# Output projection to second MLP of an encoder trunk: hand-ordered engines, another tile order, early first products

## The chip, the cores and the metric

The kernel runs on one core of one Trainium2 chip. The metric is the device time of one execution in microseconds, as the median of three runs. The core has a matrix engine (TensorE, PE in the profile, with its weight loads as PEld), a vector engine (VectorE, DVE), a scalar engine (ScalarE, ACT), a general engine (GpSimd, POOL) and an engine that issues the DMA transfers (SyncE, SP). Each of them works through its own queue of instructions in order; semaphores between them say when an operand is ready.

## The reference

Two residual layers on 1024 tokens of width 1024, in float32. Layer 0 mixes tokens by pooling, layer 1 by differential attention; each is followed by a gated MLP with a convolution over three neighbouring tokens. What is computed at the place of the change:

```python
h = h + o.reshape(b, s, 1024) @ w_o                 # output projection of the attention, residual
x = rms_norm(h, ffn_norm[1])
g, u = jnp.split(x @ w_up[1], 2, axis=-1)           # 1024 -> 2 x 2816
gc = conv_b + sum(conv_w[j] * shifted(g, j) for j in range(3))
h = h + (gelu(gc) * u) @ w_down[1]
```

## The kernel before

**Number format.** Every float32 matmul operand is split into a rounded part `hi` and a remainder `lo`, and a product is three matmuls: hi x hi, hi x lo, lo x hi. ScalarE makes `hi` (a cast), VectorE or GpSimd makes `lo` (a subtraction). All the large matmuls are 128x128 weights against 512 columns.

**The MLP's up-projection** is done in 22 units of 128 features of g and of u. A unit `j` multiplies two halves of the contraction and two halves of the tokens with seven products instead of eight (a Strassen-like scheme): products 1 to 7, twelve matmuls each, with seven token operands `x[1]` to `x[7]` (built once) and seven weight operands `w[1]` to `w[7]` (built for each unit by the generator `prep(j)`, one piece for each call of `next`). Products 1 and 2 go to one PSUM bank (`up_a`), 6, 7 and 4 to a second (`up_b`), 5 and 3 to a third (`up_c`). VectorE adds them up between the products: `u = b + g` (L511) reads the bank `up_b` after product 6, and product 7, which accumulates in the same bank, comes after it. Then come the convolution (ScalarE L536, VectorE L537 and L540) and, late, in the next unit behind its product 1, `gated(j)`: Gelu on ScalarE and two multiplications on VectorE. In `unit(j)` the products stand in the order 1, 6, 2, 7, 5, 4, 3.

**The seam.** Between the attention and that MLP stands the rest of the output projection (`wo_rest`), token tile by token tile (eight tiles of 128 tokens, in the order of `ORDER`). For each tile: load the partial sum `hs`; two halves of twelve matmuls into two banks (`wo_acc`); VectorE adds each half to `hs` (L176) and ScalarE sums the squares (L177); `rstd` makes the factor of the RMS norm (a sum, a square root on ScalarE, five small VectorE instructions); ScalarE scales the tile into `xs` (L293); TensorE transposes it in eight blocks (`tp`, L300); and `combine` builds the tile's columns of the token operands. A tile t below 4 gives columns of `x[1]` and `x[2]`. A tile t of 4 or more needs tile t - 4 as well and gives columns of `x[6]`, `x[7]`, `x[5]`, `x[4]`, `x[3]`, by three VectorE combinations (L341, L342, L343), a fourth (L345), five casts on ScalarE (L305) and five remainders, two on VectorE and three on GpSimd (L306). Product 1 of any unit needs the four tiles 0 to 3, products 6, 7, 5, 4 and 3 need all eight.

**What sets the order.** Buffers come from pools, and a scheduler places the instructions of the seam and of unit 0 on each engine by its own estimate and by the priorities written in the code. From unit 1 on a hand order holds on TensorE, VectorE and ScalarE (`manual_schedule`): there the engines take their instructions in the order in which the program writes them. GpSimd and the DMA queue are left to the scheduler.

## Time and profile before

| | |
|---|---|
| median of three runs | 2095.46 us (2094.21 to 2097.51) |
| the profiled execution | 2099.03 us, of which the span of the core is 2097.2 us |
| TensorE busy | 2010.8 us, 96% of the span |
| VectorE busy | 1561.3 us, 74% |
| ScalarE busy | 1023.4 us, 49% |
| GpSimd busy | 900.8 us, 43% |
| mean granted TensorE clock | 0.981 |

The profile's page gives shares over the whole span. The seam with its surroundings is a small part of it (about 100 us of 2097), so it has to be read from views that are cut to this stretch: busy time by windows, the chain of work that ended last, and the instructions in order of time on each engine. In the last view a row holds the start in us, the duration in us, engine, line, operation, what is written and what is read, the shapes, and in brackets the idle time of that engine just before, with what ended it.

### The profile page before, as it was taken

How to read it: one execution, taken by the hardware profiler on the slowest of the kernel's cores; microseconds unless marked ns; L12 is line 12 of the kernel's file. 1: busy time of each engine (PE TensorE's matmuls, PEld its weight loads, DVE VectorE, ACT ScalarE, POOL GpSimd, SP SyncE). 2: the span in 40 equal slices, each digit the busy share in tenths (PEclk: the TensorE clock that was granted, in tenths of full speed). 3: DMA queues.
4: the chain of work that ended last, by engine and by line, in shares of the span. 5: the costliest groups of instructions: out<-in, count | busy, mean ns of one | idle time of the engine just before them, and what ended most of it. 6: DMA issues, size and time to landing. Idle time of an engine off the chain costs nothing.

```text
span 2097.2 us, 27633 instructions
## 1 busy us (share of the span) xinstructions
PE 2010.8 (96%) x9659; PEld 1670.2 (80%) x9659; DVE 1561.3 (74%) x2278; ACT 1023.4 (49%) x1834; POOL 900.8 (43%) x689
## 2 busy tenths in 40 slices
PE   5789999999999999999999998987999999999998
PEld 5668888888888877888888886876888888888886
DVE  6877777777775658999989987768667677775665
ACT  6743333333453646666666665556333333344443
POOL 4589999996000000101110111013999999930000
PEclk8889999999999999999999999998999999999999
DMA  4225455454976422122212216243354545458663
GB/s 159 92 77 191 146 161 170 133 188 136 355 231 219 161 66 66 43 69 66 62 45 72 58 38 216 101 163 112 116 170 159 179 143 187 138 190 334 201 210 131
DMA packets 221720, 301.90 MB, mean 144 GB/s; under 512 B 17852, under 2 KB 142092, under 8 KB 218764
## 3 DMA queue, kind: packets, MB, share of 16 engines
q1 hardware_dynamic: 221580, 300.13, 43.7%
q8 instruction: 76, 1.25, 0.2%
q14 instruction: 64, 0.52, 0.1%
HBM read 196.78 MB, written 90.70 MB: 137 GB/s over the span
## 4 chain that ended last, share of the span: by engine, by line
PE 85%; DVE 8%; DMA 3%; ACT 2%; issue 1%; SPq 1%; POOL 0%; ACTq 0%; DVEq 0%; POOLq 0%
PE dn L597 19%; PE up_b L423 17%; PE up_c L423 11%; PE up_a L423 11%; PE pj L1027 7%; PE sc L1113 5%; PE pj L1069 4%; PE po L1155 3%; PE aT L1144 3%; PE pj L1240 2%; PE pp L849 1%; DVE nm L1115 1%; PE pl L829 1%; DMA kf<-t 1%; PE wo_acc L1240 1%
## 5 line engine op out<-in xcount | busy, mean ns | idle before, releaser
L1095 POOL TENSOR_TENSOR q_lo<-qt,q_hi 128x256 fp32r<-128x256 f32 x64 | 49.7, 778 | 685.6 <-ACT q_hi L1094 615.1
L381 POOL TENSOR_TENSOR w_lo<-s,w_hi 128x512 fp32r<-128x512 f32 x168 | 274.1, 1632 | 17.6 <-ACT w_hi L380 17.1
L597 PE MATMUL dn<-hnT_hi 128*128 128x512 f32 x560 | 218.1, 389 | 0.0
L597 PE MATMUL dn<-hnT_hi,hnT_lo 128*128 128x512 f32 x560 | 217.9, 389 | 0.0
L597 PE MATMUL dn<-hnT_lo,hnT_hi 128*128 128x512 f32 x560 | 217.9, 389 | 0.0
L423 PE MATMUL up_b<-x_hi,w_hi 128*128 128x512 f32 x528 | 207.0, 392 | 6.2 <-ACT x_hi L305 4.6
L423 PE MATMUL up_b<-x_lo,w_hi 128*128 128x512 f32 x528 | 206.4, 391 | 2.3 <-DVE x_lo L306 2.3
L381 POOL TENSOR_TENSOR w_lo<-raw,w_hi 128x512 fp32r<-128x512 f32 x130 | 195.1, 1501 | 30.7 <-ACT w_hi L380 26.4
L423 PE MATMUL up_b<-x_hi,w_lo 128*128 128x512 f32 x528 | 206.0, 390 | 0.0
L380 ACT CAST w_hi<-s 128x512 fp32r<-128x512 f32 x176 | 108.4, 616 | 178.7 <-PE up_b L423 87.4
L1115 DVE TENSOR_REDUCE nm<-sc 128x1 f32<-128x1024 f32 x128 | 155.8, 1217 | 15.1 <-PE sc L1113 14.1
L580 ACT CAST hnT_hi<-mst 128x1024 fp32r<-128x1024 f32 (+1 forms) x76 | 74.7, 983 | 169.1 <-PE dn L597 130.6
L581 DVE TENSOR_TENSOR hnT_lo<-mst,hnT_hi 128x1024 fp32r<-128x1024 f32 (+1 forms) x76 | 86.5, 1138 | 92.3 <-ACT hnT_hi L580 92.1
L1118 ACT ACTIVATE prob<-sc,nm 128x1024 f32<-128x1024 f32 x128 | 142.7, 1115 | 21.7 <-DVE nm L1115 11.4
L423 PE MATMUL up_a<-hnT_hi,w_hi 128*128 128x512 f32 x352 | 139.1, 395 | 1.4 <-ACT g L500 0.9
L423 PE MATMUL up_a<-hnT_lo,w_hi 128*128 128x512 f32 x352 | 138.7, 394 | 0.1
L423 PE MATMUL up_a<-hnT_hi,w_lo 128*128 128x512 f32 x352 | 138.5, 393 | 0.0
L395 POOL TENSOR_TENSOR s<-raw 128x512 f32<-128x512 f32 x84 | 133.1, 1584 | 10.4 <-DMA raw<-in_ffn_w_up_dram 4.2
L423 PE MATMUL up_c<-hnT_hi,w_lo 128*128 128x512 f32 x352 | 137.0, 389 | 0.3 <-DVE w_lo L381 0.3
L423 PE MATMUL up_c<-hnT_hi,w_hi 128*128 128x512 f32 x352 | 136.9, 389 | 0.0
L423 PE MATMUL up_c<-hnT_lo,w_hi 128*128 128x512 f32 x352 | 136.9, 389 | 0.0
L423 PEld LDWEIGHTS up_b<-x_hi,w_hi 128*128 128x128 f32 x528 | 99.5, 189 | 29.5 <-ACT x_hi L305 5.5
(296 smaller groups left out, 5455.2 us busy)
## 6 DMA issues: line engine op xcount, KB each, us to landing
raw<-in_ffn_w_up_dram SPq DMA_DIRECT2D x88, 512.0 KB, 4.3
mst<-m_dram SPq DMA_DIRECT2D x70, 512.0 KB, 5.7
wd<-in_ffn_w_down_dram SPq DMA_DIRECT2D x22, 1024.0 KB, 6.1
wd_dram<-wd SPq DMA_DIRECT2D x22, 1024.0 KB, 6.5
m_dram<-cm SPq DMA_DIRECT2D x80, 256.0 KB, 5.6
wst<-wd_dram SPq DMA_DIRECT2D x40, 512.0 KB, 4.8
m_dram<-gc SPq DMA_DIRECT2D x66, 256.0 KB, 6.3
wst<-in_ffn_w_down_dram SPq DMA_DIRECT2D x30, 512.0 KB, 6.6
```

Source lines behind the costliest of these rows:

```text
L380: A.copy(hi, src)
L381: eng.tensor_tensor(lo, src, f32(hi), ALU.subtract)
L395: eng.tensor_tensor(t, a, b, op)
L423: PE.matmul(acc, l[a][:, k], r[b][:, k], start=first and n == 0, stop=n == 11, skip_group_check=True)
L580: A.copy(h_, x)
L581: V.tensor_tensor(l_, x, f32(h_), ALU.subtract)
L597: PE.matmul(banks[t], l[:, q, cols], r[:, q], start=first and cnt == 0, stop=stop and cnt == 3 * n - 1, skip_group_check=True)
L1027: PE.matmul(acc, l[:, k % 2, h], r[:, k], start=(n == 0), stop=(n == 3 * NK - 1))
L1069: PE.matmul(acc, l[:, k % 4], r[:, k], start=(n == 0), stop=(n == 3 * NK - 1))
L1113: PE.matmul(sc[:, ns_], l[:, c], ks[:, c, ns_], start=(l is qhi), stop=(l is qlo))
L1115: V.tensor_reduce(nm, sc, AX.X, ALU.max, negate=True)
L1118: A.activation(soft[j, i][c], sc, AF.Exp, bias=nm, accum_out=sm[:, c, i:i + 1])
```

## The change

Only the seam and the first two units of the second MLP are written anew; the layer before is the same.

- The order of the tiles becomes 0 4 1 5 2 3 6 7.
- A class `Normed` holds one tile and cuts its work into `add`, `scale`, `turn`, `take`, `combine` and `combine2`. A loop over the tiles writes them with a lag: while the matmuls of tile k are issued, tile k-1 is scaled and transposed, and tile k-2 is taken from PSUM and combined.
- The hand order now begins at the seam, and holds for GpSimd too, from there to the last unit. The DMA queue is still left to the scheduler.
- Behind the last tile's matmuls stand products 1 of unit 0, then the last tile's transposes, then product 2 of unit 0 and products 1 and 2 of unit 1 (`start`); the units leave them out later. So unit 0 begins with product 6, and behind it comes product 7 at once; the same in unit 1.
- Weights: the raw weights of units 0 and 1 are loaded into the buffers `wd` and `cm`, which are free there; `w[1]` and `w[2]` of unit 0 are made during tiles 3, 6 and 7, in buffers of the pool `s`, which becomes nine buffers of 512 columns instead of four of 1024; the first two sums of unit 0's weights move from VectorE to GpSimd; the pieces of unit 1's weights come one step earlier.

```diff
-ORDER = (0, 4, 1, 5, 2, 6, 3, 7)
+ORDER = (0, 4, 1, 5, 2, 3, 6, 7)
...
-                self.s = pool(self.es_s, "s", bufs=4, side="right")
+                self.s = pool(self.es_s, "s", bufs=9, side="right")
+                self.s_shape = [P, 512]
...
+    class Normed:
+        def add(self, n, acc):
+            hs = self.h[:, n * 512:(n + 1) * 512]
+            V.tensor_tensor(hs, acc, hs, ALU.add)
+            A.activation(acc, hs, AF.Square, accum_out=self.ss[:, n:n + 1])
+        def scale(self):
+            r = rstd(self.ss)
+            self.xs = self.ar.tile("gc", [P, D], F32, "xs")
+            A.mul(self.xs, self.h, r)
+            nc.sync.dma_start(h_dram[3 * self.layer][self.tt], self.h)
...
+        def take(self):
...
+            for k in range(4):
+                A.mul(self.b12[:, k], self.pts[0][:, k], gcol[:, 2 + self.layer, k:k + 1])
+            self.gained(1, self.b22)
+        def combine(self):
+            G = nc.gpsimd
+            if self.tt < 4:
+                self.put(1, self.u, V)
+                self.put(2, self.v, G)
+                return
+            self.t3 = self.ar.tile("u2", [P, 4, P], F32, "t3")
+            V.tensor_tensor(self.t3, self.b22, self.b12, ALU.subtract)
+            V.tensor_tensor(self.b12, self.b12, self.b11, ALU.subtract)
+            V.tensor_tensor(self.b11, self.t3, self.b11, ALU.add)
+            self.put(6, self.b11, V)
+        def combine2(self):
+            G = nc.gpsimd
+            if self.tt < 4:
+                return
+            self.put(7, self.t3, G)
+            V.tensor_tensor(self.b21, self.b21, self.b11, ALU.subtract)
+            self.put(5, self.b12, V)
+            self.put(4, self.b21, G)
+            self.put(3, self.b22, G)
...
+        def start(j, i):
+            if i == 1:
+                a = ar.tile("ps_dn" if man and j == 1 else "ps_up", [P, 512], F32, "up_a")
+                product(j, 1, a, True)
+                g = ar.tile("g", [P, S], F32, "g")
+                A.copy(half(g, 0), a)
+                pre[j, 1] = a, g
+            else:
+                product(j, 2, pre[j, 1][0], False)
+                pre[j, 2] = True
...
-    each_with_lag(ORDER, wo_rest, lambda: next(mlp))
+    man.enter_context(tc.manual_schedule(engines=ENGINES | {mybir.EngineType.Pool}))
...
+    for k, tt in enumerate(ORDER):
+        p, pp = at(k - 1), at(k - 2)
+        acc = wo_half(tt, 0)
+        if pp:
+            pp.take()
+        if p:
+            p.scale()
+        tiles[tt].add(0, acc)
+        acc = wo_half(tt, 1)
+        if pp:
+            pp.combine()
+        tiles[tt].add(1, acc)
+        if pp:
+            pp.combine2()
+        if p:
+            p.turn()
+        if k == 0:
+            api["load"](0)
+            first, after = api["prep"](0), api["prep"](1)
+            api["next"] = after
+        elif k == 2:
+            api["load"](1)
+        elif k > 4:
+            next(first)
+    p, pp = at(7), at(6)
+    api["start"](0, 1)
+    pp.take()
+    p.scale()
+    pp.combine()
+    p.turn()
+    next(after)
+    api["start"](0, 2)
+    p.take()
+    p.combine()
+    next(first)
+    api["start"](1, 1)
+    pp.combine2()
+    p.combine2()
+    for _ in first:
+        pass
+    api["start"](1, 2)
```

How this moves the instructions shows at three places. In the rows below `rt` is the square root of the norm, `wo_acc,ss<-hs` the sum of squares of one half, `x_hi` and `hnT_hi` are casts of token operands, `w_hi` of weight operands, `b`, `t` and `xf` the tiles that are combined.

ScalarE in the middle of the tile loop, before: the square root of a tile stands between single casts.

```order
L177 ACTIVATE wo_acc,ss<-hs 128x512
L293 ACTIVATE xs<-hs,rs_r 128x1024
L305 CAST x_hi<-xf 128x4x128
L305 CAST hnT_hi_69<-b_13784 128x4x128
L305 CAST x_hi<-xf 128x4x128
L177 ACTIVATE wo_acc,ss<-hs 128x512
L305 CAST hnT_hi_67<-xf 128x4x128
L191 ACTIVATE rt<-ss,eps 128x1
L305 CAST hnT_hi_67<-xf 128x4x128
L177 ACTIVATE wo_acc,ss<-hs 128x512
L293 ACTIVATE xs<-hs,rs_r 128x1024
```

The same engine after, at tile 3: between the last sum of squares and the square root of the same tile now stand the four casts of tile 5 and one cast of a weight.

```order
L365 ACTIVATE wo_acc,ss<-hs 128x512
L383 CAST x_hi<-xf 128x4x128
L365 ACTIVATE wo_acc,ss<-hs 128x512
L383 CAST x_hi<-t_13862 128x4x128
L383 CAST hnT_hi_69<-b_13825 128x4x128
L383 CAST x_hi<-xf 128x4x128
L383 CAST hnT_hi_69<-b_13826 128x4x128
L459 CAST w_hi<-raw_13535 128x512
L191 ACTIVATE rt<-ss,eps 128x1
L370 ACTIVATE xs<-hs,rs_r 128x1024
```

ScalarE at the last tile, before: the copy `g<-up_a` of unit 0's product 1 stands behind the last tile's square root and scaling.

```order
L177 ACTIVATE wo_acc,ss<-hs 128x512 x2
L305 CAST hnT_hi_67<-xf 128x4x128 x2
L191 ACTIVATE rt<-ss,eps 128x1
L293 ACTIVATE xs<-hs,rs_r 128x1024
L332 ACTIVATE b_14074<-tp,gcol 128x128 x4
L500 COPY g<-up_a 128x512
```

After: that copy, and four reads of tile 6's transposes, stand ahead of the last tile's square root.

```order
L365 ACTIVATE wo_acc,ss<-hs 128x512
L578 COPY g<-up_a 128x512
L403 ACTIVATE b_14046<-tp,gcol 128x128 x4
L191 ACTIVATE rt<-ss,eps 128x1
L370 ACTIVATE xs<-hs,rs_r 128x1024
L383 CAST x_hi<-xf 128x4x128
```

VectorE at unit 0, before: the sum `u<-up_b,g` stands ahead of the last weight remainder, and the sum `s` and remainders of a single tile are ahead of it.

```order
L345 TENSOR_TENSOR xf<-xf 128x512
L306 TENSOR_TENSOR x_lo<-xf,x_hi 128x4x128
L306 TENSOR_TENSOR hnT_lo_70<-b_14074,hnT_hi_69 128x4x128
L381 TENSOR_TENSOR w_lo<-s,w_hi 128x512
L395 TENSOR_TENSOR s<-raw,s 128x512
L381 TENSOR_TENSOR w_lo<-s,w_hi 128x512
L381 TENSOR_TENSOR w_lo<-raw,w_hi 128x512
L511 TENSOR_TENSOR u_14156<-up_b,g 128x512
L381 TENSOR_TENSOR w_lo<-s,w_hi 128x512
```

After: ten instructions of the token operands of tiles 6 and 7 and of all of unit 0's remaining weights stand ahead of it.

```order
L423 TENSOR_TENSOR xf<-xf 128x512
L384 TENSOR_TENSOR hnT_lo_70<-b_14046,hnT_hi_69 128x4x128
L423 TENSOR_TENSOR xf<-xf 128x512
L384 TENSOR_TENSOR hnT_lo_70<-b_14104,hnT_hi_69 128x4x128
L474 TENSOR_TENSOR s<-raw_13535 128x512
L460 TENSOR_TENSOR w_lo<-s,w_hi 128x512 x2
L460 TENSOR_TENSOR w_lo<-raw_13535,w_hi 128x512
L474 TENSOR_TENSOR s<-raw_13535,s 128x512
L460 TENSOR_TENSOR w_lo<-s,w_hi 128x512
L608 TENSOR_TENSOR u_14207<-up_b,g 128x512
```

More of the change, by code (lines that the diff above doesn't have):

```diff
@@ L362, in each_with_lag, with ffn @@
         late()
-    def ffn(layer, ar, tail, extra=None):
+    def ffn(layer, ar, tail, extra=None, api=None, man=None):
         G = nc.gpsimd
@@ L495, in unit @@
                 load_down(1)
-            a = ar.tile("ps_up", [P, 512], F32, "up_a")
-            product(j, 1, a, True)
-            g = ar.tile("g", [P, S], F32, "g")
-            A.copy(half(g, 0), a)
+            if (j, 1) not in pre:
+                start(j, 1)
+            a, g = pre[j, 1]
             if late:
@@ L513, in unit @@
             step()
-            product(j, 2, a, False)
+            if (j, 2) not in pre:
+                start(j, 2)
             next(side, None)
@@ L710, in down_all @@
             return ends[2:]
-        load(0)
-        first = prep(0)
-        next(first)
-        if layer:
-            next(first)
-        yield
-        load(1)
-        for _ in first:
-            pass
-        unit(0, prep(1))
-        load(2)
-        with tc.manual_schedule(engines=ENGINES):
+        if api is not None:
+            api.update(load=load, prep=prep, start=start)
+            yield
+            unit(0, api["next"])
+            load(2)
             for j in range(1, NF):
@@ L726, in ffn @@
                 load(j + 2)
+            man.close()
+        else:
+            load(0)
+            first = prep(0)
+            next(first)
+            yield
+            load(1)
+            for _ in first:
+                pass
+            unit(0, prep(1))
+            load(2)
+            with tc.manual_schedule(engines=ENGINES):
+                for j in range(1, NF):
+                    unit(j, prep(j + 1))
+                    load(j + 2)
         ar.open_down()
```

93 lines of the change are left out of this document (70 added, 23 removed).

## The prediction

> **What bounds the kernel now.** I first cut the busy time into windows around the seam, from the first `wo_acc` matmul (1386.73) on.
>
> ```profile
> core 0: us, PE busy (x) PEld busy (x) DVE busy (x) ACT busy (x) POOL busy (x), PEclk, DMA share, GB/s
> 1386.73:1451.00 64.27, 54.38 (x250) 43.90 (x248) 49.11 (x96) 39.93 (x85) 20.17 (x14) 0.92 0.40 131
> 1451.00:1487.34 36.34, 32.68 (x129) 24.71 (x129) 22.25 (x32) 18.23 (x31) 23.18 (x16) 0.92 0.29 87
> 1487.34:1525.00 37.66, 37.66 (x166) 31.20 (x167) 27.05 (x27) 13.65 (x20) 37.03 (x24) 1.00 0.47 153
> 1900.00:2000.00 100.00, 100.00 (x443) 82.80 (x442) 58.47 (x65) 42.65 (x54) 0.00 (x0) 1.00 0.70 245
> ```
>
> From 1487.34 on TensorE is busy without a gap, at full clock; before that it idles and is slowed. The seam can therefore only move the time by moving that moment. The chain of waits and TensorE's instructions in order of time show what it is:
>
> ```profile
> 1487.34 3.02 PE up_b L423 x12
> 1490.35 2.72 PE up_c L423 x12
> ```
>
> ```profile
> 1404.28 1.09 PE L300 MATMUL tp<-ident,xs 128*128 128x128 f32 x8 [0.75 <-ACT xs L293]
> 1405.13 0.48 PE L1240 MATMUL wo_acc<-wo_l,hnT_lo 128*128 128x512 f32 x1
> 1436.77 1.97 PE L300 MATMUL tp<-ident,xs 128*128 128x128 f32 x8 [2.67 <-ACT xs L293]
> 1448.42 1.97 PE L300 MATMUL tp<-ident,xs 128*128 128x128 f32 x8 [4.15 <-ACT xs L293]
> 1452.44 0.63 PE L423 MATMUL up_a<-hnT_hi,w_lo 128*128 128x512 f32 x1
> 1452.87 0.63 PE L423 MATMUL up_a<-hnT_hi,w_hi 128*128 128x512 f32 x1
> 1487.34 0.50 PE L423 MATMUL up_b<-x_hi,w_hi 128*128 128x512 f32 x1 [0.34 <-DVE u L511]
> ```
>
> The last row is product 7 of unit 1, released by `u` (L511) of unit 1. Call this moment R; from the first `wo_acc` matmul it is 1487.34 - 1386.73 = 100.6 us away. Before R stand 192 matmuls of `wo_acc`, ten products of twelve (unit 0's seven and products 1, 6, 2 of unit 1) and 64 transposes. A product takes 2.72 us, and eight transposes hold TensorE for 0.85 (1404.28 to 1405.13): 26 x 2.72 + 8 x 0.85 = 77.5. So 23.1 us are lost: 9.9 + 3.7 = 13.6 idle (the windows), and 9.5 in stretches at half clock, where matmuls follow each other at 0.43 (1452.44, 1452.87) instead of 0.227 us.
>
> **What the change does to this.** The matmuls before R are the same: the units still have ten products before product 7 of unit 1, in another order (products 1 and 2 of both units come first). If nothing were lost, the gain would be 23 us. I place the new order's instructions one after the other on each engine, with these durations:
>
> ```profile
> 1396.95 0.16 DVE L197 SCALAR_TENSOR_TENSOR rs_q<-rs_p,rt 128x1 f32<-128x1 f32 x1
> 1397.15 0.16 DVE L199 SCALAR_TENSOR_TENSOR rs_r<-rs_q,rt 128x1 f32<-128x1 f32 x1
> ...
> 1463.59 0.68 DVE L306 TENSOR_TENSOR x_lo<-xf,x_hi 128x512 fp32r<-128x512 f32 x1
> 1464.19 0.68 DVE L306 TENSOR_TENSOR hnT_lo<-b,hnT_hi 128x512 fp32r<-128x512 f32 x1
> ```
>
> ```profile
> 1428.11 0.62 ACT L305 CAST x_hi<-xf 128x512 fp32r<-128x512 f32 x1 [1.08 <-DVE xf L343]
> 1428.63 0.61 ACT L305 CAST hnT_hi<-b 128x512 fp32r<-128x512 f32 x1
> 1434.44 0.60 ACT L177 ACTIVATE wo_acc<-hs 128x512 f32<-128x512 f32 x1 [0.71 <-DVE hs L176]
> 1435.57 1.15 ACT L293 ACTIVATE xs<-hs,rs_r 128x1024 f32<-128x1024 f32 x1 [0.41 <-DVE rs_r L199]
> 1437.98 1.14 ACT L332 ACTIVATE b<-tp,gcol 128x128 f32<-128x128 f32 x4 [0.76 <-PE tp L300]
> 1442.34 0.29 ACT L191 ACTIVATE rt<-ss,eps 128x1 f32<-128x1 f32 x1 [1.74 <-DVE ss L189]
> ```
>
> ```profile
> 1424.46 1.30 POOL L306 TENSOR_TENSOR hnT_lo<-b,hnT_hi 128x512 fp32r<-128x512 f32 x1 [5.15 <-ACT hnT_hi L305]
> 1425.73 1.80 POOL L306 TENSOR_TENSOR x_lo<-t,x_hi 128x512 fp32r<-128x512 f32 x1
> ...
> 1470.21 1.29 POOL L395 TENSOR_TENSOR s<-raw 128x512 f32<-128x512 f32 x1 [4.18 <-DMA raw<-in_ffn_w_up_dram]
> ...
> 1473.96 1.30 POOL L395 TENSOR_TENSOR s<-raw 128x512 f32<-128x512 f32 x1
> 1475.21 1.30 POOL L395 TENSOR_TENSOR s<-raw,s 128x512 f32<-128x512 f32 x1
> ```
>
> ```profile
> 1425.70 0.68 DVE L342 TENSOR_TENSOR b<-b,xf 128x512 f32<-128x512 f32 x1
> 1426.42 1.66 DVE L343 TENSOR_TENSOR xf<-t,xf 128x512 f32<-128x512 f32 x1
> ```
>
> So in a row VectorE takes 0.60 for a 512-column instruction and 0.20 for a small one, ScalarE 0.52 for a cast, 0.64 for a square with its read-out (estimate from the 0.60), GpSimd 1.25. The last two fences show one more price: a VectorE instruction with both inputs in SBUF and a GpSimd instruction do not run together. GpSimd's at 1425.73 took 1.80 beside VectorE's L342, and VectorE's L343, issued at 1426.42, ended only 0.55 after GpSimd's end at 1427.53. They take turns; a turn of both is 1.25 + 0.60 = 1.85.
>
> *The tile loop.* Between a tile's last matmul and its own transposes TensorE has 0.85 + 5.44 = 6.3 us of other work. For tiles 0, 4, 1, 2 and 6 the chain add, square, sum, root, five small instructions, scaling fits or nearly fits into this (stalls 0.2 and 0.5 by the same placing). For tile 5 it does not, since tile 4's `combine` and `combine2` stand in it: 1.4 until VectorE is through with the remainder of `x[6]`, add 0.7, square 0.65, two casts 1.1, 0.8 until GpSimd's remainder ends, VectorE's remainder and two reads 1.8, sum 0.2, root and reciprocal 0.55, 0.65 until GpSimd's next remainder ends and three small ones 0.6, scaling 1.2: 9.6, a stall of 3.3. For tile 3 the same, with a weight cast (0.5) and one more turn of both (1.85): 12.0, a stall of 5.7. Sum of the loop: 9.7.
>
> *The last tile.* Product 1 of unit 0 starts 1.0 late, because tile 3's remainder stands behind an add. Then tile 7's transposes: the square root waits on ScalarE behind the copy of that product, which only starts 0.2 after the product's end: 0.2 + 0.5 copy + 1.1 reads of tile 6 + 0.3 root + 0.8 small ones + 1.2 scaling = 4.1. Together 5.1. Before, the root stood ahead of the copy.
>
> *Product 7 of unit 0.* Time 0 is the end of tile 7's transposes. TensorE has products 2, 1', 2' (those of unit 1) and 6: until 10.9. Product 7 needs VectorE's `u` of unit 0. VectorE: reads of tile 7 and three combinations until 5.4, behind a GpSimd turn (ScalarE's reads end at 2.4, GpSimd's weight remainder at 3.4), cast and remainder of `x[6]` 6.7, weight 6 at 7.3. Then the ten instructions of the last listing above, beside GpSimd's six remainders of tiles 6 and 7 and two sums of unit 1: the first 0.6, eight turns 14.8: 22.7; the cast of the last weight 0.8, its remainder 0.6, `u` 0.7: 24.8. TensorE waits 13.9. In the order before, `u` of unit 0 was not last of the row, and GpSimd had no work for unit 1 then, because unit 1's raw weights had not arrived (the 4.18 at 1470.21). That wait for a DMA goes, and its work comes in the worst place.
>
> *Product 7 of unit 1.* It needs `u` of unit 1, which stands behind the Gelu of unit 0:
>
> ```profile
> 1476.16 0.69 DVE L533 TENSOR_TENSOR g<-up_b,g 128x512 f32<-128x512 f32 x1 [2.03 <-PE up_b L423]
> 1478.65 1.45 DVE L537 SCALAR_TENSOR_TENSOR gc<-g,convp,gc 128x1023 f32<-128x1023 f32 x1 [1.80 <-ACT gc L536]
> 1480.62 1.71 DVE L540 SCALAR_TENSOR_TENSOR gc<-g,convp,gc 128x1023 f32<-128x1023 f32 x1
> 1485.08 0.69 DVE L475 TENSOR_TENSOR gc<-up_a,gc 128x512 f32<-128x512 f32 x1 [2.75 <-ACT gc L474]
> 1486.60 0.68 DVE L511 TENSOR_TENSOR u<-up_b,g 128x512 f32<-128x512 f32 x1
> ```
>
> From the reading of product 4 (1476.16) to R are 11.2 us. TensorE covered them with four products (10.9), hence the idle 0.34. In the new order two of the four, 1 and 2 of unit 1, are already done; products 3 and 6 cover 5.4. A wait of 5.8 takes the place.
>
> *The DMA queue* I cost at nothing. Unit 0's raw weights take the place of an early load of the same size, unit 1's go out while the first tile runs; a tile's `hs` follows the store of the tile three places ahead:
>
> ```profile
> 1393.96 0.32 SPq L294 DMA_DIRECT2D h_dram<-hs  x1
> 1398.52 0.32 SPq L1361 DMA_DIRECT2D hs<-h_dram  x1
> ```
>
> 4.6 for the store and about as much for the load are under the 16 us between the two tiles' uses; with unit 1's loads beside them the margin is still some 4 us.
>
> *Sum.* Lost after: 9.7 + 5.1 + 13.9 + 5.8 = 34.5, at full clock. Before: 23.1, slow clock included: + 11.4. The clock comes on top. After the idle of 2.67 the transposes took 1.97, not 1.09, and after that of 4.15 the slow stretch lasted from 1448.42 past 1452.87. Three of the new waits (5.7, 13.9, 5.8) are followed by work that R or the end hangs on; from the trace's 9.5 us, lost in three such stretches (at the seam's start and behind the two idles), one costs 3.2. The bounds are 0 and 9.5; I take 4, below the middle, since part falls into waits that are there anyway. Result: + 15.4. The profiled execution took 2099.03 (its span 2097.2 and 1.8 around it), so 2114.4; it lay 3.6 above the median of the runs, 2095.46. On the median: 2111.
>
> On the clock the Trainium skill ("TensorE: Matmul & The Clock Gate", Part 1) says that the clock falls to half after an idle window of about 3.4 us, and returns after as long a busy one. The trace disagrees on the first: 2.67 us were enough. By the page a wait costs an estimated 1.7 us, three cost 5.1, and the sum would be 2112 on the median.
>
> **Rivals.**
> - *Faster.* The place is VectorE's row ahead of unit 0's `u`. If VectorE and GpSimd hardly held each other there (as the rows at 1463.59 and 1464.19, back to back at 0.60), `u` would come at 7.3 + 6.0 + 0.8 + 0.7 = 14.8, the tile loop would lose some 5 less, and lost time is 9.7 - 5 + 5.1 + 3.9 + 5.8 = 19.5; where the ten are also ready early enough that TensorE does not wait for `u` at all, 15.6, which is 7.5 less than now: 2088. It decides from a wait under 3 us there. Against it: the rows at 1425.73 and 1426.42. Chance 0.09.
> - *No change.* The stalls of the loop are only those of the loop before (2.67 and 4.15), and the row ahead of `u` is held half as often: 34.5 - 2.9 - 7.4 = 24.2, 1.1 more than now, and little clock: 2097. Chance 0.13.
> - *GpSimd becomes the bound.* Fourteen of its instructions lie between tile 7 and the last sum of unit 1, whose cast stands on ScalarE ahead of unit 0's convolution. At 1.80 each (1425.73) they end at 7.9 + 25.2 = 33.1, as late as product 4 at 24.8 + 8.2 = 33.0; with the cast 1.4 more than the forecast, and the whole 9.5 of the clock: 11.4 + 1.4 + 9.5 = 22.3, or 2118. Chance 0.15.
> - *The forecast*, between 2102 and 2118: 0.63.
>
> **Numbers.** 0.2% or 4.2 us is about what a measurement of this kernel can tell from no change. Slower by more: 0.63 + 0.15 = 0.78; within: 0.12; faster: 0.10, 0.01 of the second rival counted there. The range reaches down through the no-change case to 2094 and up to 2119, just over the GpSimd case: it leaves out the faster case and the upper half of that one, under 2 in 10.
>
> **What would show it.** Right: in the profile after, TensorE busy without a gap only from about 1500 on; an idle of 10 us or more ahead of an `up_b` matmul, released by `u`; a second of about 6; idles at `tp` of 3 to 6, released by `xs`; VectorE instructions of 1.7 to 1.9 us ahead of `u`. Wrong: the ten instructions at 0.6 to 0.7 each, or the four products ahead of product 6 following at once on tile 6's transposes. The forecast falls if the wait ahead of unit 0's product 7 is under 5 us.

## The result, and the profile after

The changed kernel takes 2112.14 us (median of four runs, 2109.24 to 2116.04), the kernel before 2094.84 in the same session: a ratio of 1.0079 (95% interval 1.0065 to 1.0094), 17.3 us slower. The forecast was 2111.

The profiled execution lasted 2109.24 with a span of 2107.5, which is only 10.3 more than the span before. The difference is in front of the seam: the first `wo_acc` matmul came 7.6 earlier than in the profile of before, although nothing was changed there.

The first `wo_acc` matmul and the first `dn` matmul, TensorE in order of time, before:

```profile
1386.73 1.05 PE L1240 MATMUL wo_acc<-wo_l,hnT_hi 128*128 128x512 f32 x2
1879.15 0.39 PE L597 MATMUL dn<-hnT_hi 128*128 128x512 f32 x1
```

and after, with every idle of TensorE in between up to R (product 7 of unit 1):

```profile
1379.12 0.63 PE L1346 MATMUL wo_acc<-wo_l,hnT_hi 128*128 128x512 f32 x2
...
1412.23 1.10 PE L378 MATMUL tp<-ident,xs 128*128 128x128 f32 x8 [2.98 <-ACT xs L370]
1430.72 1.97 PE L378 MATMUL tp<-ident,xs 128*128 128x128 f32 x8 [3.96 <-ACT xs L370]
1446.24 1.09 PE L378 MATMUL tp<-ident,xs 128*128 128x128 f32 x8 [3.90 <-ACT xs L370]
1455.12 0.50 PE L508 MATMUL up_a<-hnT_hi,w_hi 128*128 128x512 f32 x1 [0.72 <-ACT g L578]
1471.41 0.77 PE L508 MATMUL up_b<-x_hi,w_hi 128*128 128x512 f32 x1 [10.55 <-DVE u L608]
1492.04 0.77 PE L508 MATMUL up_b<-x_hi,w_hi 128*128 128x512 f32 x1 [5.25 <-DVE u L608]
...
1889.66 0.39 PE L695 MATMUL dn<-hnT_hi 128*128 128x512 f32 x1
```

So two stretches are to be compared. I call them the seam (first `wo_acc` to R) and the units (R to the first `dn`). The seam took 1492.04 - 1379.12 = 112.9 where it took 100.6: + 12.3. The units took 397.6 where they took 391.8: + 5.8. Together 18.1; what lies behind `dn` is alike to 0.2 (217.8 against 218.0). That the two medians differ by 17.3 fits this, and not the 10.3 of the spans.

Busy time by windows, after:

```profile
core 0: us, PE busy (x) PEld busy (x) DVE busy (x) ACT busy (x) POOL busy (x), PEclk, DMA share, GB/s
1379.12:1451.00 71.88, 61.03 (x279) 50.09 (x278) 46.20 (x100) 40.59 (x90) 21.16 (x16) 0.93 0.43 139
1451.00:1492.04 41.04, 24.52 (x100) 19.24 (x99) 25.68 (x26) 15.16 (x24) 24.36 (x17) 0.87 0.16 52
1525.00:1600.00 75.00, 75.00 (x329) 61.08 (x328) 56.88 (x52) 26.58 (x40) 63.58 (x43) 1.00 0.49 162
```

Of the seam's 112.9, 77.5 are work; 10.85 + 16.52 = 27.4 are idle, and the remaining 8.0 went in half clock. Before it was 13.6 and 9.5. The last row looks like full work at full clock, and yet is not without a gap. The gaps are too small for the busy column; the chain of waits shows them, one in the product 7 of each unit (2.96 us for a product that takes 2.72):

```profile
1548.70 2.72 PE up_a L508 x12
1551.42 2.96 PE up_b L508 x12
...
1570.70 2.95 PE up_b L508 x12
```

The unit lasts 1570.70 - 1551.42 = 19.28, where seven products are 19.04. Asked for the waits of the weight loads in the units, the trace after names `u` nineteen times (6.5 us in all, 0.5 the longest); before, it names none behind R:

```profile
PEld up_b L508 <- DVE u L608: 6.5, 19, 0.5
```

What makes `u` late are two VectorE instructions of the chain ahead of it: the first part of the convolution (L537 in the kernel before, L635 in the changed one) and the second multiplication of `gated` (L476 and L561). One unit before, VectorE and the GpSimd instructions that begin ahead of each of the two:

```profile
1535.92 1.31 DVE L537 SCALAR_TENSOR_TENSOR gc<-g,convp,gc 128x1023 f32<-128x1023 f32 x1 [1.31 <-ACT gc L536]
1541.54 1.01 DVE L476 TENSOR_TENSOR gc<-u,gc 128x512 f32<-128x512 f32 x1
```

```profile
1534.85 1.29 POOL L381 TENSOR_TENSOR w_lo<-s,w_hi 128x512 fp32r<-128x512 f32 x1
1540.70 1.30 POOL L395 TENSOR_TENSOR s<-raw 128x512 f32<-128x512 f32 x1
```

and one unit after:

```profile
1542.59 2.29 DVE L635 SCALAR_TENSOR_TENSOR gc<-g,convp,gc 128x1023 f32<-128x1023 f32 x1 [1.32 <-ACT gc L634]
1548.92 1.78 DVE L561 TENSOR_TENSOR gc<-u,gc 128x512 f32<-128x512 f32 x1
```

```profile
1542.50 1.30 POOL L460 TENSOR_TENSOR w_lo<-raw,w_hi 128x512 fp32r<-128x512 f32 x1
1548.86 1.29 POOL L460 TENSOR_TENSOR w_lo<-raw,w_hi 128x512 fp32r<-128x512 f32 x1 [0.57 <-ACT w_hi L459]
```

Before, GpSimd's instructions began 1.07 and 0.84 ahead of VectorE's; after, they begin 0.09 and 0.06 ahead, and VectorE's take 0.98 and 0.77 longer. The unit shown is one of the shortest before: over 18 units behind R, L537 took 1.28 to 2.24, and L476 took 0.99 to 1.79, in eleven of them 1.78 or 1.79 as after. What never came before is both of them long in one unit. Their sum was 2.27 to 3.66, without a wait for `u`; after, it is 4.03 to 4.20 in the 19 units that wait, by 0.32 to 0.48 each, and 2.94 in the last one, which doesn't wait.

### The profile page after: what moved, and what is told of

Same layout as the page of the kernel before. It is cut to its first block, busy times and chain, and to the rows that moved or that the text cites. A ratio compares the mean times of both kernels' runs of the same rounds, so it can differ in the third digit from the quotient of the medians.

```text
span 2107.5 us, 27591 instructions
## 1 busy us (share of the span) xinstructions
PE 2014.7 (96%) x9659; PEld 1670.6 (79%) x9659; DVE 1571.4 (75%) x2276; ACT 1021.5 (48%) x1834; POOL 875.5 (42%) x691
## 4 chain that ended last, share of the span: by engine, by line
PE 85%; DVE 7%; ACT 3%; DMA 2%; issue 1%; SPq 1%; POOL 0%; ACTq 0%; DVEq 0%; POOLq 0%
PE dn L695 19%; PE up_b L508 17%; PE up_c L508 11%; PE up_a L508 11%; PE pj L1133 7%; PE sc L1219 5%; PE pj L1175 4%; PE po L1261 3%; PE aT L1250 2%; PE pj L1346 2%; PE wo_acc L1346 1%; PE pp L955 1%; DVE nm L1221 1%; PE pl L935 1%; ACT prob L1224 1%
## 5 line engine op out<-in xcount | busy, mean ns | idle before, releaser
L460 POOL TENSOR_TENSOR w_lo<-s,w_hi 128x512 fp32r<-128x512 f32 x168 | 248.1, 1482 | 57.4 <-ACT w_hi L459 57.2
L460 POOL TENSOR_TENSOR w_lo<-raw,w_hi 128x512 fp32r<-128x512 f32 x130 | 188.3, 1449 | 44.2 <-ACT w_hi L459 44.2
L508 PEld LDWEIGHTS up_b<-x_hi,w_hi 128*128 128x128 f32 x528 | 100.4, 190 | 49.1 <-ACT w_hi L459 10.9
```

The lines of the kernel that those rows point to most:

```text
L460: eng.tensor_tensor(lo, src, f32(hi), ALU.subtract)
L508: PE.matmul(acc, l[a][:, k], r[b][:, k], start=first and n == 0, stop=n == 11, skip_group_check=True)
```

## The experiments

All ran against the kernel before, which took 2090.5 to 2091.1 in these sessions. Seam and units in us, from the trace of one execution of each run:

| run | median us | ratio to before (95%) | seam | units |
|---|---|---|---|---|
| before (first profile) | | 1 | 100.6 | 391.8 |
| changed kernel again | 2111.12 | 1.0097 (1.0082 to 1.0111) | 112.9 | 396.8 |
| before, GpSimd by hand in the units | 2098.03 | 1.0040 (1.0027 to 1.0052) | 100.5 | 398.9 |
| GpSimd to the scheduler from unit 1 | 2146.58 | 1.0271 (1.0257 to 1.0285) | 114.7 | 433.8 |
| two weight steps moved in the units | 2133.65 | 1.0202 (1.0188 to 1.0217) | 114.0 | 418.3 |
| unit 0's weights stepped, with unit 1's | 2113.16 | 1.0112 (1.0096 to 1.0127) | 116.9 | 398.0 |
| unit 0's weights stepped, unit 1's behind | 2106.39 | 1.0075 (1.0061 to 1.0089) | 110.8 | 397.2 |
| root ahead of reads and remainders | 2113.62 | 1.0116 (1.0102 to 1.0130) | 117.7 | 397.6 |
| root ahead of remainders | 2108.94 | 1.0084 (1.0069 to 1.0098) | 110.7 | 397.6 |
| unit 1 without early products | 2109.52 | 1.0086 (1.0072 to 1.0100) | 115.4 | 396.1 |
| remainders to VectorE | 2109.06 | 1.0082 (1.0069 to 1.0095) | 115.2 | 395.9 |
| old tile order | 2111.87 | 1.0099 (1.0085 to 1.0113) | 115.3 | 397.7 |
| three edits together | 2100.34 | 1.0046 (1.0032 to 1.0060) | 106.0 | 396.3 |

The seam varies by itself. Two runs that leave the program of the seam as it is (GpSimd to the scheduler from unit 1; two weight steps moved) show 114.7 and 114.0, where the changed kernel shows 112.9 twice; in both, tile 3's stall is 5.25 or 5.26 instead of 3.96. So a seam that is 2 us longer or shorter says little more than this, and the waits have to be read beside it. Of the edits to the seam, only the three together have an interval of the ratio that lies apart from that of the changed kernel (1.0082 to 1.0111).

My theory: the 12.3 at the seam are what the prediction named (stalls behind the root, the row ahead of `u`, the Gelu without cover), and of the 5.8 in the units, 1.2 are product 7 of unit 1 at half clock behind its wait, and 4.6 are GpSimd's handmade order. The rivals: the units are late because unit 1 enters late; and at the seam there is one bound, so that any edit only moves the waits.

**The changed kernel again.**

> The changed kernel itself, as the measure for the three others of this call. Both theories expect the ratio of the result, 1.008 (1.0065 to 1.0094): some 17 us over the kernel before. If the seam and the units are the whole of it, its trace shows 112.9 us from the first wo_acc matmul to product 7 of unit 1, give or take 1.5, and 397.8 from there to the first dn matmul.

As expected: the ratio's interval overlaps that of the result, the seam is 112.9 again, and the units 396.8. The median is 20.6 above the kernel before, where the two stretches give 17.2; the rest lies elsewhere or in the spread of the runs (2108.09 to 2115.49). The units show where the wait for `u` begins. In the first three of this trace the sum of L635 and L561 is 3.07, 3.63 and 3.85, and nothing waits; in the next 16 it is 4.05 to 4.07, and each has a wait of 0.33 to 0.35.

**GpSimd by hand in the kernel before.** Only the engines of the hand order change:

```diff
-        with tc.manual_schedule(engines=ENGINES):
+        with tc.manual_schedule(engines=ENGINES | ({mybir.EngineType.Pool} if layer else set())):
```

> The kernel before, with GpSimd put in program order from unit 1 of the second MLP on, and nothing else. Theory A (GpSimd's handmade order costs the units): product 7 of most units waits 0.2 to 0.5 us for u, a unit takes 19.27, and the time rises by about 20 x 0.23 = 4.6, to 2099.5 or so from 2095. Rival B (the late entry at the seam does it): the seam is the old one, so the units stay at 19.04 and the time at 2095.

The seam stays at 100.5, the units rise by 7.1 to 398.9, the time by 0.40%. Waits of the weight loads (two of the 21 lie ahead of R, in a stretch that begins at the seam; behind R they are 19 and 7.8 us), and VectorE in one unit:

```profile
PEld up_b L423 <- DVE u L511: 8.8, 21, 1.4
```

```profile
1607.66 2.30 DVE L537 SCALAR_TENSOR_TENSOR gc<-g,convp,gc 128x1023 f32<-128x1023 f32 x1 [1.31 <-ACT gc L536]
1614.00 1.78 DVE L476 TENSOR_TENSOR gc<-u,gc 128x512 f32<-128x512 f32 x1
```

2.30 and 1.78 with the old seam: the handmade order of GpSimd does it, not the late entry. It costs more here than I had expected (4.6), since unit 2 waits 1.21 and 0.95 besides.

**GpSimd back to the scheduler.** The hand order of GpSimd ends behind unit 0:

```diff
-            for j in range(1, NF):
-                unit(j, prep(j + 1))
-                load(j + 2)
             man.close()
+            with tc.manual_schedule(engines=ENGINES):
+                for j in range(1, NF):
+                    unit(j, prep(j + 1))
+                    load(j + 2)
```

> The changed kernel, but GpSimd's order is by hand only up to unit 0 of the second MLP; from unit 1 on it is left to the scheduler, as before the change. In the changed kernel's trace product 7 of every unit from 2 to 21 waits about 0.33 us for VectorE's u (L608), and a unit takes 19.27 us where it took 19.04. Theory A: it is GpSimd's handmade order that does this (its remainders fall on the convolution and the Gelu of VectorE); then the units go back to 19.04, the 0.33 waits go, and the time falls by 19 x 0.23 = 4.2: 2108 where the changed kernel has 2112. Rival B: the units are late because unit 1 enters its Gelu late at the seam and never catches up, whatever GpSimd's order; then the waits of 0.33 stay and the time stays at 2112. Up to the start of product 7 of unit 1 (R) nothing changes by either.

Both theories missed: the units take 433.8. Waits of the weight loads in the units, and GpSimd in order of time:

```profile
PEld up_c L508 <- POOL w_lo L460: 28.3, 14, 3.1
```

```profile
1617.90 1.29 POOL L474 TENSOR_TENSOR s<-raw 128x512 f32<-128x512 f32 x1 [5.78 <-DMA raw<-in_ffn_w_up_dram]
```

The scheduler now gives GpSimd another order than before the change; it stands still for a raw weight and its remainders come late for TensorE. Why that load comes late I did not follow. So this run says nothing on the two theories, only that "left to the scheduler" is not one order.

**Two weight steps moved.** In units 1 to 21:

```diff
-            step()
+            moved = man and j
+            if not moved:
+                step()
             b = ar.tile("ps_up", [P, 512], F32, "up_b")
             product(j, 6, b, True)
...
             next(side, None)
             step()
+            if moved:
+                step()
...
-            step()
+            if not moved:
+                step()
             gc = ar.tile("gc", [P, S], F32, "gc")
             A.activation(gc, g, AF.Identity, bias=cv[:, 3, j:j + 1], scale=cv[:, 1, j:j + 1])
             V.scalar_tensor_tensor(gc[:, 1:], g[:, :S - 1], cv[:, 0, j:j + 1], gc[:, 1:], ALU.mult, ALU.add)
+            if moved:
+                step()
```

> The changed kernel, with GpSimd in program order as it is, but in units 1 to 21 two of the weight steps are written elsewhere: the one ahead of product 6 behind u, and the one ahead of the convolution behind its first VectorE instruction (L635 there). Theory (in the units it is not the handmade order as such that costs 0.23 a unit but two collisions: GpSimd's remainder starts 0.1 ahead of L635, which takes 2.29 instead of 1.3, and another falls on L561, 1.78 instead of 1.0, so that u comes late for product 7): L635 goes back to 1.3 or L561 to 1.0 to 1.2, product 7 no longer waits, a unit takes 19.04 and the time falls by about 4. Rival: GpSimd's instructions only move on to other VectorE instructions of the same chain; 0.2 to 0.3 a unit stays and the time is within 1.5 of the changed kernel.

The convolution's collision goes (1.28), and yet the units take 21.5 us more than in the changed kernel of that session. VectorE's convolution and ScalarE behind it, in one unit:

```profile
1611.05 1.28 DVE L640 SCALAR_TENSOR_TENSOR gc<-g,convp,gc 128x1023 f32<-128x1023 f32 x1 [1.31 <-ACT gc L639]
```

```profile
1615.75 0.62 ACT L459 CAST w_hi<-s 128x512 fp32r<-128x512 f32 x1 [4.23 <-POOL s L474]
...
1616.76 1.06 ACT L559 ACTIVATE gc<-gc 128x1024 f32<-128x1024 f32 x1
```

The Gelu (L559) stands behind a cast that waits 4.23 for GpSimd's sum, and product 7 waits 1.35 for `u` in a unit, although the sum of L640 (the convolution here) and L561 is only 3.06. So collisions are one way in which GpSimd's order makes `u` late, and a cast on ScalarE behind a GpSimd sum is another; a better place for the steps was not found.

**Unit 0's weights behind `u`.** First try: each step of unit 0 (`both`) advances the weights of unit 0 and those of unit 1.

```diff
-    for _ in first:
-        pass
     api["start"](1, 2)
+    api["next"] = both(first, after)
```

> The changed kernel, but the last four weights of unit 0 (w7, w5, w4, w3) are not all made ahead of unit 0; they go out in unit 0's own steps, behind u. Theory (VectorE's row ahead of u is what product 7 of unit 0 waits for): six of the instructions ahead of u go, at a turn of 1.70 each; u comes about when product 6 ends, and product 7 waits only for w7 (sum, cast, remainder, some 4 us) instead of 10.55. R moves 6 ahead and the time falls to about 2106. Rival: the row only moves; the same remainders then stand ahead of the readings and the convolution of unit 0, the wait of 5.25 ahead of unit 1's product 7 grows by as much, and the time stays at 2112 within 2.

Neither: product 7 waits 7.86 now for a cast, unit 1's wait is 7.36, and the seam is 4 longer. TensorE, and ScalarE at that place:

```profile
1469.73 0.79 PE L508 MATMUL up_b<-x_hi,w_hi 128*128 128x512 f32 x1 [7.86 <-ACT w_hi L459]
```

```profile
1468.54 1.66 ACT L459 CAST w_hi<-s 128x512 fp32r<-128x512 f32 x3 [7.13 <-POOL s L474]
```

ScalarE had unit 1's cast in front, which waits for GpSimd's sum; unit 0's `w[7]` stood behind it. Second try: the seven steps of unit 0 (`shared`) advance unit 0's weights in the first four, unit 1's in the last six:

```diff
-    for _ in first:
-        pass
+    next(first)
     api["start"](1, 2)
+    api["next"] = shared(first, after)
```

> The changed kernel, but w5, w4 and w3 of unit 0 are made in unit 0's own steps behind u, and unit 1's weights one step behind unit 0's (so that no sum of GpSimd for unit 1 stands ahead of unit 0's w7 on ScalarE, as it did in the run before). Theory (the row of VectorE ahead of u is what product 7 waits for): four turns of 1.70 go, the wait of 10.55 becomes about 4, R comes 6 earlier and the time falls by 5 to 7 against the changed kernel. Rival (GpSimd's row of six remainders and two sums is the bound behind it): product 7 of unit 0 starts earlier, but the wait ahead of unit 1's product 7 or a weight of unit 1 grows by the same; within 2 of the changed kernel.

```profile
1468.79 0.77 PE L508 MATMUL up_b<-x_hi,w_hi 128*128 128x512 f32 x1 [4.15 <-DVE u L608]
1491.68 0.76 PE L508 MATMUL up_b<-x_hi,w_hi 128*128 128x512 f32 x1 [6.20 <-DVE u L608]
```

The first wait falls from 10.55 to 4.15, as the theory had it; the second grows by 0.95, and tile 3's stall was 5.26 here, not 3.96. So the row ahead of `u` was the cause of that wait. What it pays alone is less sure: R comes 2.1 earlier, the median is 4.7 lower, and the intervals of the two ratios overlap.

**The root ahead.** First try: the root and the scaling of a tile ahead of the reads (`take`) and of `combine2` of the tiles before, `combine2` one tile later (`p3` is the tile three places back; `at(5)` is tile 3, which has no `combine2`).

```diff
         acc = wo_half(tt, 0)
+        if p:
+            p.scale()
+        if p3:
+            p3.combine2()
         if pp:
             pp.take()
-        if p:
-            p.scale()
...
-        if pp:
-            pp.combine2()
...
     p, pp = at(7), at(6)
+    p.scale()
+    at(5).combine2()
     api["start"](0, 1)
     pp.take()
-    p.scale()
```

> The changed kernel, but in the tile loop and behind it the square root, the small instructions and the scaling of a tile stand ahead of the reads and remainders of the tiles before it (combine2 follows one turn later). Theory (the waits of 2.98, 3.96 and 3.90 ahead of the transposes of tiles 5, 3 and 7 come from the remainders that stand ahead of the root): these three waits go, with them some 3 us at half clock; tile 7's transposes come 10 earlier, VectorE's row behind them moves along, and R and the end come 8 to 12 earlier: about 2102. Rival: VectorE's and GpSimd's row of remainders is a bound of its own, since it is now put off; u of unit 0 comes no earlier, the wait ahead of product 7 grows from 10.55 to 18 or more, and the time stays within 3 of 2112.

```profile
1430.95 1.94 PE L378 MATMUL tp<-ident,xs 128*128 128x128 f32 x8 [5.40 <-DVE xf L388]
```

A new wait took the place of the old: tile 3's transposes wait for their PSUM bank, which the reads (L388) give back too late now. Second try, with `take` first again and `combine2` put off. Behind the loop the edit also writes product 1 of unit 0, with the copy that reads it, behind the last tile's scaling.

```diff
         if pp:
             pp.take()
         if p:
             p.scale()
+        if p3:
+            p3.combine2()
...
-        if pp:
-            pp.combine2()
...
     p, pp = at(7), at(6)
-    api["start"](0, 1)
     pp.take()
     p.scale()
+    at(5).combine2()
+    api["start"](0, 1)
```

> The changed kernel, but a tile's last remainders (combine2) are put off until the next tile's root and scaling are out; the reads of the transposes keep their place. (The run before put the reads off too, so the transposes waited for their bank: that wait of 5.4 took the place of the others.) Theory (the waits of 2.98, 3.96 and 3.90 at the transposes come from the remainders that stand ahead of the root): they fall under 1.5 each, the last tile's transposes come 7 to 10 earlier and the time falls by 6 to 10. Rival (VectorE and GpSimd are the bound behind the last tile, with the same row put off): u of unit 0 comes no earlier than 92.3 after the first wo_acc matmul, its wait grows to 18, and the time stays within 2 of the changed kernel.

```profile
1416.43 1.09 PE L378 MATMUL tp<-ident,xs 128*128 128x128 f32 x8 [2.98 <-ACT xs L370]
1424.15 1.09 PE L378 MATMUL tp<-ident,xs 128*128 128x128 f32 x8 [1.16 <-ACT xs L370]
1434.41 1.09 PE L378 MATMUL tp<-ident,xs 128*128 128x128 f32 x8 [3.70 <-ACT xs L370]
1441.65 1.09 PE L378 MATMUL tp<-ident,xs 128*128 128x128 f32 x8 [1.35 <-ACT xs L370]
1466.48 0.76 PE L508 MATMUL up_b<-x_hi,w_hi 128*128 128x512 f32 x1 [10.73 <-DVE u L608]
```

```profile
1440.45 1.15 ACT L370 ACTIVATE xs<-hs,rs_r 128x1024 f32<-128x1024 f32 x1 [1.51 <-DVE rs_r L199]
1441.51 0.57 ACT L578 COPY g<-up_a 128x512 f32<-128x512 f32 x1
```

The four stalls belong to tiles 2, 3, 6 and 7. The 2.98 of tile 5 now stands at tile 2, and the 3.96 of tile 3 has become 3.70 at tile 6: each one tile later, as `combine2` is. So these two do come from the remainders of `combine2`, and putting them off only moves them on. Tile 7's stall falls from 3.90 to 1.35 for another reason than the theory's, since nothing of `combine2` was moved there: the copy `g<-up_a`, which stood ahead of its square root, now stands behind its scaling. The sum is 9.2 instead of 10.8. The last tile's transposes come 1.9 earlier, and `u` and R come 2.1 and 2.2 earlier, with the same wait of 10.73. So the row moves along with the last tile (against the rival); the size was missed (expected 6 to 10; the median is 2.2 lower, with overlapping intervals).

**Unit 1 without early products.**

```diff
-    api["start"](1, 1)
...
-    api["start"](1, 2)
```

> The changed kernel without unit 1's early products: products 1 and 2 of unit 1 stand in unit 1 again, behind unit 0. Theory (what sets R is the moment of u of unit 0, and from there five products, the Gelu of unit 0 and u of unit 1; two products more in the middle only fill one wait or the other): the wait of 5.25 ahead of product 7 of unit 1 falls under 1, the wait ahead of product 7 of unit 0 grows from 10.55 to 16, R stays at 112 to 113 after the first wo_acc matmul, and the time stays within 3 of 2111. Rival (the early products of unit 1 are what costs: they take the Gelu's cover away): the wait of 5.25 goes without a return, R comes 5 to 6 earlier with its slow clock, and the time falls by 6 or more, to a ratio of 1.006 to 1.007 over the kernel before.

```profile
1471.64 0.77 PE L508 MATMUL up_b<-x_hi,w_hi 128*128 128x512 f32 x1 [11.46 <-DVE u L608]
1494.41 0.50 PE L508 MATMUL up_b<-x_hi,w_hi 128*128 128x512 f32 x1 [0.63 <-DVE u L608]
```

The rival falls. The Gelu's wait is nearly gone (0.63); ahead of product 7 of unit 0 stand 11.46 and, ahead of product 6, 2.66 for a cast, together 14.1 where the theory had 16; and R comes 2.5 later, not 5 earlier. Idle time is 25.7 instead of 27.4, the half clock 12.2 instead of 8.0. The two early products of unit 1 fill one wait or the other, as the theory had it; that R would stay was missed by the half clock.

**Remainders to VectorE.**

```diff
-            self.put(7, self.t3, G)
+            self.put(7, self.t3, V)
...
-            self.put(4, self.b21, G)
-            self.put(3, self.b22, G)
+            self.put(4, self.b21, V)
+            self.put(3, self.b22, V)
...
-            w[4] = parts(g2, eng)
+            w[4] = parts(g2, V if man else eng)
```

> The changed kernel with two prices moved, each read in its own stretch of the trace. At the seam the remainders of x[7], x[4] and x[3] are VectorE's and not GpSimd's. Theory (the two engines take turns, 1.70 a pair): the row ahead of u of unit 0 has 14 instructions at 0.6 and a turn or two, 10 to 11 us, where it took 14; the wait of 10.55 becomes 6 to 8, and R comes 2 to 4 earlier than 112.9. Rival (GpSimd's help is worth its turns): the row takes 14 or more and the stalls at the transposes grow by a us each; R comes at 114 or later. In units 1 to 21 the remainder of w4 is VectorE's, between the reading of product 4 and the convolution, where VectorE waits 1.3 for ScalarE. Theory (GpSimd's remainders on L635 and L561 make u late for product 7): a unit takes 19.04 instead of 19.27, the stretch from R to the first dn matmul falls from 397.8 to 394. Rival: the next instruction of GpSimd takes the same place; 397.8 stays.

```profile
1463.41 0.68 DVE L423 TENSOR_TENSOR xf<-xf 128x512 f32<-128x512 f32 x1
1464.01 0.68 DVE L384 TENSOR_TENSOR hnT_lo<-b,hnT_hi 128x512 fp32r<-128x512 f32 x1
```

```profile
1471.98 0.77 PE L508 MATMUL up_b<-x_hi,w_hi 128*128 128x512 f32 x1 [8.23 <-DVE u L608]
```

Alone, VectorE's instructions follow each other at 0.60; the wait is 2.3 shorter. But the first stall of the loop is 1.0 longer, TensorE reaches the last tile later, and the seam is 2.3 longer (115.2), as the rival had it. In the units the waits for `u` are 9 instead of 16 (the changed kernel again): L635 now takes 1.52 in every second unit, where the sum with L561 is 3.30 and nothing waits, and 2.30 in the others, where the sum is 4.08 and the wait 0.35 or 0.36. The stretch is only 0.9 shorter, where the theory had 3.8; the two profiles of the changed kernel differ by as much (397.6 and 396.8).

**The old tile order** in the changed kernel. Product 1 of unit 0 then stands ahead of tile 3's columns of `x[1]`, so this run leaves tile 3's part out of that one product: it times the order and does not compute the kernel's result.

```diff
-ORDER = (0, 4, 1, 5, 2, 3, 6, 7)
+ORDER = (0, 4, 1, 5, 2, 6, 3, 7)
```

> The changed kernel with the tile order of before, 0 4 1 5 2 6 3 7: one number changed. Theory (a stall comes behind each tile that is combined with another, whatever its place): the stalls of 3 to 5 stand behind the tile that follows the combine2 of tiles 4, 5 and 6, so the loop has one such stall more; but tile 6's combinations then lie in the loop and not behind the last tile, so that the row ahead of u is three remainders of VectorE and three of GpSimd shorter: the stall of 4 to 5 is paid back by a wait at product 7 that is 4 to 6 shorter; the time stays within 3 of 2111. Rival (the new order itself costs, since it heaps two combined tiles at the end): the wait falls by 5 and no stall takes its place; the time falls by 5 or more.

```profile
1450.53 1.97 PE L378 MATMUL tp<-ident,xs 128*128 128x128 f32 x8 [7.70 <-ACT xs L370]
1472.56 0.77 PE L508 MATMUL up_b<-x_hi,w_hi 128*128 128x512 f32 x1 [6.12 <-DVE u L608]
```

As the theory had it: the wait ahead of product 7 is 4.4 shorter, the last tile's stall 3.8 longer, the time the same. So the new tile order is not what costs.

**Three edits together**: unit 0's weights behind `u` (second try), `combine2` put off (second try, with product 1 of unit 0 behind the scaling), `w[4]`'s remainder on VectorE.

> The changed kernel with the three edits that each took something off: unit 0's w5, w4 and w3 behind u; combine2 put off until the next tile's root is out; the remainder of w4 on VectorE in all units. Theory (the stalls at the transposes, the row ahead of u and GpSimd's place in the units are three costs one behind the other): from the first wo_acc matmul to product 7 of unit 1 it takes 107 to 109 us (112.9 less 2 to 3 and 2.2), from there to the first dn matmul 396 (397 less 1 to 1.6), and the time is 6 to 8 under the changed kernel, a ratio of 1.005 to 1.007 over the kernel before: faster than the changed kernel, not faster than before. Rival (they share one bound, the work of VectorE and GpSimd behind the last tile): the seam stays at 110.5 or more and the time within 5 of the changed kernel, 1.0075 or more.

```profile
1462.36 0.77 PE L508 MATMUL up_b<-x_hi,w_hi 128*128 128x512 f32 x1 [4.31 <-DVE u L608]
1484.47 0.76 PE L508 MATMUL up_b<-x_hi,w_hi 128*128 128x512 f32 x1 [6.54 <-DVE u L608]
```

The seam is 106.0, 6.9 shorter than in the changed kernel, a little more than the sum expected; the time is 10.8 lower (2100.34 against 2111.12), more than the 7.4 which the two stretches give; the rest is not accounted for. The interval of the ratio (1.0032 to 1.0060) lies below that of the changed kernel, so this gain is clear, and the rival (one shared bound) falls: the costs at the seam lie one behind the other. It is still 0.46% slower than the kernel before, and no version here was faster than that.

## Why the prediction was right, point by point

The sum: predicted + 15.4, all of it before R. Measured: + 12.3 before R and + 5.8 behind it. The mechanism at the seam came as forecast (stalls at `tp`, the row of turns ahead of `u`, the wait for the Gelu). That 2111 lies within 1.2 of the median of 2112.14 is in part luck: idle time was forecast 7.1 too long, half clock 4.0 too short, and 5.8 behind R were left out.

- *Only moving R moves the time.* This step failed. I read from the windows before (TensorE without a gap from R on) that nothing would change there, and did not price that GpSimd's handmade order holds for all 22 units. It costs 4.6 in the units; with the old seam the same order cost 7.1. The other 1.2 of the 5.8 are product 7 of unit 1, which began at half clock behind its wait of 5.25 (4.25 to the next product, instead of 3.01).
- *The tile loop, 9.7.* Measured 2.98 + 3.96 = 6.9. Tile 5: 3.3 predicted, 2.98. Tile 3: 5.7 predicted, 3.96 to 5.26 in the runs that keep this order. The two small stalls did not come. That the stalls come from `combine2` is shown by the run that puts it off: they moved on by a tile.
- *The last tile, 5.1.* Measured 3.90 ahead of the transposes (4.1 predicted); the late product 1 (1.0) did not come; instead 0.72 ahead of unit 1's product 2, for the copy of its product 1. That the copy ahead of the square root is the main part of the 3.90 is shown by the run that moved it: 1.35.
- *Product 7 of unit 0, 13.9.* Measured 10.55. Yet `u` came when predicted: 24.8 after the end of tile 7's transposes, measured 1471.26 - 1447.09 = 24.2. What was wrong is TensorE's side: I had it there at 10.9, it came at 13.8, since the first nine matmuls of product 2 of unit 0 followed each other at half clock (1447.09 to 1450.82) and product 2 of unit 1 waited for the copy. TensorE's own delays cost nothing there, since VectorE ended the wait.
- *A turn of VectorE and GpSimd, 1.85.* Measured 1.70. The row ahead of `u`, and GpSimd beside it:

```profile
1457.44 1.78 DVE L423 TENSOR_TENSOR xf<-xf 128x512 f32<-128x512 f32 x1
1459.14 1.78 DVE L384 TENSOR_TENSOR hnT_lo<-b,hnT_hi 128x512 fp32r<-128x512 f32 x1
...
1470.58 0.68 DVE L608 TENSOR_TENSOR u<-up_b,g 128x512 f32<-128x512 f32 x1
```

```profile
1458.63 1.75 POOL L384 TENSOR_TENSOR hnT_lo<-b,hnT_hi 128x512 fp32r<-128x512 f32 x1
1460.34 1.71 POOL L384 TENSOR_TENSOR x_lo<-t,x_hi 128x512 fp32r<-128x512 f32 x1
```

  They start 1.70 apart on both engines. The Trainium skill ("SBUF — State Buffer", section "Who interferes with whom") says that a VectorE instruction with two inputs in SBUF contends with a GpSimd instruction that reads SBUF, that issue order decides which of them is blocked, and that, outside the 2-port modes, one with a single SBUF input doesn't contend. The trace agrees: 1.78 against 0.68 for `u`, which reads one input from PSUM and ran beside a GpSimd instruction begun at 1470.53.
- *Product 7 of unit 1, 5.8.* Measured 5.25. That the early products cause it is right as far as that wait goes; taking them back does not shorten the seam (115.4).
- *The clock, + 4 on 34.5 lost.* Idle was 27.4, not 34.5; half clock took 8.0, not 4. Two errors of 7.1 and 4.0 against each other. The Trainium skill ("TensorE: Matmul & The Clock Gate", Part 1) puts the drop behind at least one idle window of about 3.4 us, and says that the window runs freely. On the length the trace disagrees: behind the idle of 2.98, matmuls already followed each other at 0.42 (1413.98, 1414.40). On the free window it agrees: after the idle of 3.96 the transposes took 1.97, after that of 3.90 they took 1.09 and only the matmuls behind them were slow, and in the run with two weight steps moved the same tile's idle of 3.91 was followed by 1.97. So it is not the idle's length alone.
- *DMA at nothing, GpSimd as the bound:* the first held (no wait for a raw weight shows at the seam), the second case did not come: `u` of unit 1 waited for the Gelu, not for a sum.

## What to carry to other kernels

A hand order that is extended to one engine more acts in every pass in which it holds, not only where it was meant; here it cost 4.6 to 7.1 us there. Price the steady part as well, and look for it in the waits of the weight loads, since 0.3 us a unit doesn't show in busy time. Read every unit and not one: a single unit would have blamed two instructions, and the waits go by their sum. Where two engines take turns and a third waits for one of them, moving work between them moves the wait; what helped was to put behind the awaited instruction what is not needed for it. And compare stretches between fixed points of the program, not whole spans: here the spans differed by 10.3, the stretches by 18.1 and the medians by 17.3.

## What the runs showed of the hardware that was not expected

How long a VectorE instruction with two inputs in SBUF is held follows from how far ahead of it GpSimd's began. The first part of the convolution (128x1023) took, in the kernel before, 1.28 us where GpSimd's instruction had begun 1.21 ahead, 1.47 at 0.92, 1.89 at 0.49 and 2.24 at 0.14; in the changed kernel, 2.25 to 2.29 at 0.07 to 0.12. `u`, with one input in PSUM, took 0.68 in these units although a GpSimd instruction had begun some 0.5 ahead. So where GpSimd stands, 1 us earlier or later, changes the period of a loop that is otherwise bound by TensorE (19.28 instead of 19.04). Small instructions are held too: L197 (128x1), 0.16 elsewhere, took 1.19 at 1428.05 with a GpSimd instruction begun at 1427.96, in the chain ahead of tile 3's transposes.
